# One inference step of a hybrid attention/RG-LRU layer on one core: values placed between zeros, a new order of the first loads and of the middle, and the last gate products on VectorE

## The chip, the cores and the metric

The kernel runs on one core of one Trainium2 chip. The core's engines are TensorE (PE, with its weight loads shown as PEld), VectorE (DVE), ScalarE (ACT), GpSimd (POOL) and SyncE (SP), which issues most DMAs. The metric is the device time of one execution in microseconds. Three runs of the kernel before took 758.29, 759.57 and 760.28 us, median 759.57.

## The reference, cut to what matters

One layer is computed for 512 latent tokens and 128 context tokens, all in float32. With `h` the normed and modulated input:

```
z = h @ w_in                                  # q, k, v, lx (LRU input), lg
attn  = windowed GQA (8 query heads, 2 key/value heads of 64, sink logit, 2-D rope);
        latent tokens also see the 128 cached context keys and values
xc    = conv4(lx);  r, ig = sigmoid(xc @ w_r), sigmoid(xc @ w_i)   # per direction
a     = exp(8 r log_sigmoid(lam));  u = sqrt(1 - a^2) * ig * xc
lru   = (forward scan of h = a h + u  +  backward scan) * gelu(lg)
x     = x + gate1 * rmsnorm([attn, lru] @ w_out)
h2    = rmsnorm(x) * (1 + scale2) + shift2
f     = relu(h2 @ w_up)^2 @ w_down
x     = x + gate2 * rmsnorm(f)
```

The outputs are both `x`, and the new keys, values and LRU states of the context. The attention step that the change touches is `einsum('bkgqs,bskd->bqkgd', p, v)`: for each of the two key/value heads, softmax weights times values, summed over blocks of 128 keys.

## The kernel before

The 640 tokens are columns; d_model is eight tiles of 128 partitions. A float32 product of large matrices is made of three products of rounded operands: each operand is split into a high part and a low part (`split`, `low` L231, `weight` L262), and high x high, high x low and low x high add up in one PSUM bank. Transposes, attention's weight-times-value products and the small products of the modulation stay plain float32.

The work comes in stages. A string START (L72) is a list of the first steps in strict order: loads of the input, of modulation weights (D, Q) and of input-projection weights (W), norms, modulation and the first input-projection tiles (m, h, b, z). A second string ORDER (L80) lists the middle: z are further tiles of the input projection, g0 to g3 the gates of the four LRU channel blocks (`lru_gates` L620: four 128x128 weights on two halves of 322 columns, each read out of PSUM by a sigmoid on ACT), x their decay (`lru_decay` L655: exp, tanh and square on ACT), q their scans (`lru_scan` L674: square root on ACT, then two scans on DVE), rope and keys the keys, vt the values (`do_values` L847), qs the query stacks, and u{g}{qb} ten attention units, one for each key/value head pair group g and query block qb. Then come the output projection, and the MLP: sixteen pairs of hidden tiles by a Strassen-like scheme of seven products (`up7` L1176), each followed by its part of the down projection (`down` L1262). At the last down, each of the five token tiles is finished (`out_part` L1239, `out_tile` L1249): square for the norm on ACT, product with the gate, scaled add to the residual, and the store.

ACT needs a table load whenever the kind of function changes: sigmoid, exp with tanh, square root. A table WORK (L38) gives for each kind of small work a string of letters, one per instance: a is ACT, d is DVE, p is POOL, s is a negated copy on ACT with an accumulating DMA issued by POOL, m a mixture. Behind START the order on each engine comes from the scheduler, which takes ORDER as priorities; the engines then run their lists in that order and wait for each other by semaphores. PSUM has eight banks: three z, two s, two t and one pv.

A unit (L772) makes scores for its keys on 64-row tiles, softmax on DVE and ACT, and then for each block of 128 keys four transposes into a bank t, one copy out of it, and the products with the values (L816). There the values of a block (`vblock` L765) are two tiles of 128x64: the product for half 0 writes PSUM partitions 0 to 63, that for half 1 partitions 64 to 127, each with 256 columns. A float32 product leaves two matmul records in the trace, one for each pass. Over ten units there are 30 such blocks.

Of the kernel before, what the change touches and what calls it, by code (L numbers as in the profile page):

```python
# [15 lines left out]
ALU = mybir.AluOpType  # L16
# [19 lines left out]


WORK = {  # L38
    "h_lo": "dpdddpdd",
    "lx_weight_lo": "pddp",  # L40
    "z_weight_hi": "ddddddaaaaaaaa",
    "z_weight_lo": "ddpppdddspdssd",
    "z_out": "aamadmamdmammm",
    "gate_weight_lo": "dddd",
    "lru_x_lo": "pdpp",
    "gated_x": "dpdpppdp",
    "gated_input": "dddppppp",
    "directions": "dppp",
    "rope_sin": "ppddd",
    "rope_cos": "pddpp",  # L50
    "rope_sum": "pdddd",
    "q_hi": "aaad",
    "q_lo": "dppd",
    "softmax_scale": "ammdamaddd",
    "softmax_turned": "daaaadaadadaddaadadddaaaaadaaadddaddadad",
    "attention_hi": "adaaaadaaa",
    "gelu_lo": "sssp",
    "w_out_hi": "ddaaddad",
    "w_out_lo": "ppppdpsdspppddpd",
    "norm_scaled": "adaaa",  # L60
    "h_whole": "dddddddd",
    "plain_lo": "pppp",
    "up_sums": "ddpd",
    "up_lo": "ddddddp",
    "up_square": "a",
    "down_lo": "pddp",
    "modulated": "daddddddddd",
}

START = """  # L72
    X3 X1 X0 Q1 X2 X4 X5 X6 Q3 Q0 X7 Q2 Q4 Q5 Q7 Da Q6 pt D1 a0 D0 tr dg a1 a2 a3 Db W0 D2 rb ac D3 m0 m1 b0 h0
    W1 m2 h1 b1 z00 b2 m3 z01 h2 h3 z20 z11 z30 W2 Ds z10 z31 b3 z21 bc z02 z22 s0 W3 m5 m4 z12 h4 z03 z32 m6
    z40 z13 s1 Dt z42 h5 z52 m7 h6 z41 z23 s2 h7 z51 t0 t1 z62 z33 t2 t3 z50 z43 s3 z61 z60 z72 sc z71 z53 tc
    z70 z63 z73
"""


ORDER = """  # L80
    z4 g0 z1 g1 m4 x0 rope m5 q0 keys x1 g2 z0 z5 q1 g3 qs0 vt x2 m6 z3 x3 q2 q3 qs1 m8 u00 z2 u01 m7 qs2 qs3
    u04 u11 z10 u12 m9 u03 g1d u10 u02 u13 z11 u14 z13 z12 l1 l2 l0 l3
"""
MOD_BANKS, GATE_BANKS, LX_BANKS = "tszztz", "sssz", "zszz"
MIX_BANKS, TURN_BANK = ("t", "t", "s", "s"), "z"

PLAIN = 2
SUMS = 0
RING = (0, 1, 7, 6, 2, 4, 3, 8, 5)
X1K, TK, KC = 0, (2, 4, 5), (4, 2)  # L90


class Arena:
# [59 lines left out]
def hybrid_step(ctx, tc, xT, xN, vecs, ropeT, ckT, cv, gw, modw, modg, win, wout, wup, wdown,  # L153
# [65 lines left out]
    def on(work, i):  # L219
        return engines[WORK[work][i]]  # L220
# [502 lines left out]
        evac(z_tile(ft), z.f, eng=WORK["z_out"][ft])  # L723
        return z

    vt, vb = blk.alloc(keep=True), blk.alloc(keep=True)
    ctxk = blk.alloc(keep=True)
    sp.dma_start(out=ctxk.f[:, :P], in_=ckT)
    sp.dma_start(out=vt.f[:, TOK - P : TOK], in_=cv)


    def keys(zk):

# [29 lines left out]
             (384, 384, 8, (2, 3, 4)), (768, 128, 9, (5,))]  # L763

    def vblock(b, g):  # L765
        if b == 5:
            return vb.f[:, 64 * g : 64 * g + 64]
        return vt.f[:, b * P + 64 * g : b * P + 64 * g + 64]

    ucol = [0]  # L770

    def unit(g, qb, qs):  # L772
        k0, n, m0, vbs = UNITS[qb]
        qc = slice(qb * P, (qb + 1) * P)
# [24 lines left out]
        dve.tensor_tensor(out=dn, in0=mn, in1=psink[:, 4 * g : 4 * g + 4], op=ALU.add)  # L799
        table("exp", act.activation(dn, dn, AF.Exp))  # L800
        dve.tensor_tensor(out=dn, in0=dn, in1=rs, op=ALU.add)
        dve.reciprocal(dn, dn)
        for j in range(4):
            if WORK["softmax_scale"][un] == "a" or (WORK["softmax_scale"][un] == "m" and j % 2):
                act.activation(S[j].f[:, :n], S[j].f[:, :n], AF.Copy, scale=dn[:, j : j + 1])
            else:
                dve.tensor_scalar(S[j].f[:, :n], S[j].f[:, :n], dn[:, j : j + 1], None, ALU.mult)
        pv = bank("pv")
        for b, vbk in enumerate(vbs):
            tr = bank("t")  # L810
            for pos, j in enumerate((0, 2, 1, 3)):
                pe.transpose(tr[:, pos * P : (pos + 1) * P], S[j].f[:, b * P : (b + 1) * P], idn)
            pt = blk.alloc()
            copy_on("softmax_turned", 4 * un + b, pt.f[:, :512], tr)
            for half in range(2):
                pe.matmul(pv[64 * half : 64 * half + 64, 0:256], vblock(vbk, half),  # L816
                          pt.f[:, 256 * half : 256 * half + 256], start=(b == 0), stop=(b == len(vbs) - 1))
            pt.free()
        for s in S:
            s.free()  # L820
        src = pv[:, 0:256].rearrange("p (k c) -> p k c", c=P)
        hv, lv = mixed[1][:, 2 * g : 2 * g + 2, qc], mixed[2][:, 2 * g : 2 * g + 2, qc]
        copy_on("attention_hi", un, hv.bitcast(F32R), src)
        dve.tensor_tensor(out=lv.bitcast(F32R), in0=src, in1=hv, op=ALU.subtract)
# [22 lines left out]
    def do_values():  # L847
        zv = zb[FT_V]
        for b0 in range(2):
            tr = bank("t")  # L850
            n = 4 if b0 == 0 else 1
            for b in range(n):
                pe.transpose(tr[:, b * P : (b + 1) * P], zv.f[:, (4 * b0 + b) * P : (4 * b0 + b + 1) * P], idn)
            dve.tensor_copy(vt.f[:, :512] if b0 == 0 else vb.f[:, :P], tr[:, : n * P])
        zv.free()
        sp.dma_start(out=v_o, in_=vb.f[:, :P])

    def do_unit(g, qb):
# [380 lines left out]
    def out_part(t, n, c, s):  # L1239
# [4 lines left out]
        if t == 4:  # L1244
            dve.tensor_tensor(out=g3b[1].f[:, c], in0=ac[t][:, c], in1=g3b[1].f[:, c], op=ALU.mult)
        else:
            pool.tensor_tensor(out=ac[t][:, c], in0=ac[t][:, c], in1=g3b[0].f[:, c], op=ALU.mult)

    def out_tile(t, s):  # L1249
        dve.tensor_tensor(out=s[:, 0:1], in0=s[:, 0:1], in1=s[:, 1:2], op=ALU.add)  # L1250
# [174 lines left out]
```

## Time and profile before

| what | value |
|---|---|
| median of three runs | 759.57 us |
| profiled execution, its own time | 758.07 us |
| its span | 754.8 us |
| PE busy | 715.4 us, 95% |
| DVE busy | 575.6 us, 76% |
| ACT busy | 397.3 us, 53% |
| POOL busy | 218.2 us, 29% |
| matmul records / table loads in the program | 4036 / 15 |
| DMA read / written | 89.34 / 5.40 MB |

The shares are averages over stages that differ. 0 to 28 us is the start, 28 to 93 modulation and input projection, 93 to 160 the LRU gates with the rest of the projection, 160 to 264 the attention units, 264 to 345 the output projection and the second norm, 345 to 740 the MLP, and the rest the last tiles' norms. A stage is read by the wait that ends last in it, not by the average. Start times in a timeline tell more than durations where TensorE is full, because matmuls overlap.

### The profile page before, as it was taken

The page shows a single profiled execution, that of the slowest core. Times are in us where ns is not written, and L with a number is a line of the kernel's source. Part 1 is how long each engine was busy: PE and PEld are TensorE (multiplying, and loading weights), DVE is VectorE, ACT ScalarE, POOL GpSimd, SP SyncE. Part 2 cuts the span into 40 slices and gives each one's busy share as a digit, 9 for nine tenths or more (in the row PEclk, how much of TensorE's full clock was granted, in tenths as well). Part 3 has the DMA queues.
Part 4 walks back from the last instruction along what each step waited for, and adds up shares of the span by engine and source line. Part 5 has one row for each costly group of instructions (what it writes and reads, how often), then busy time and mean ns, then how long its engine had stood idle before and what let it go on. Part 6 is the DMA issues. An engine that isn't in the chain of part 4 may idle for free. (4 is left out here: it accounts for less than half of the span.)

```text
span 754.8 us, 10989 instructions
## 1 busy us (share of the span) xinstructions
PE 715.4 (95%) x4036; PEld 593.0 (79%) x4036; DVE 575.6 (76%) x1011; ACT 397.3 (53%) x794; POOL 218.2 (29%) x179
## 2 busy tenths in 40 slices
PE   6899987999999999989999999999999999999992
PEld 2468876666666778789898998898899889888982
DVE  3736578776575648999999998786878778778568
ACT  6315598956555649746355345453544345344522
POOL 2302347641120343700321132033113303321323
PEclk9999999999999999999999999999999999999997
DMA  8953252757100797503423442033123203313403
GB/s 331 408 164 126 74 168 73 254 151 185 39 30 29 191 252 273 167 34 102 152 89 108 168 165 80 35 112 112 30 82 112 85 29 112 112 44 125 140 28 139
DMA packets 36837, 96.43 MB, mean 128 GB/s; under 512 B 11776, under 2 KB 12464, under 8 KB 36784
## 3 DMA queue, kind: packets, MB, share of 16 engines
q1 hardware_dynamic: 35760, 92.66, 36.3%
q0 software_dynamic: 1024, 3.08, 2.2%
q8 instruction: 31, 0.51, 0.3%
q14 instruction: 22, 0.18, 0.1%
HBM read 89.34 MB, written 5.40 MB: 126 GB/s over the span
## 5 line engine op out<-in xcount | busy, mean ns | idle before, releaser
L207 PE MATMUL ps_z<-rnd 128*128 128x320 f32 (+5 forms) x1756 | 298.8, 317 | 10.3 <-ACT big L207 4.6
L207 PEld LDWEIGHTS ps_z<-rnd 128*128 128x128 f32 x1756 | 270.2, 190 | 35.2 <-issue 11.0
L207 ACT CAST rnd<-big 128x512 fp32r<-128x512 f32 (+4 forms) x218 | 140.9, 657 | 221.7 <-PE ps_z L207 66.0
L1075 POOL TENSOR_TENSOR rnd<-big,rnd 128x512 fp32r<-128x512 f32 x54 | 84.2, 1572 | 277.3 <-ACT rnd L207 165.2
L207 ACT ACTIVATE big<-big 128x320 f32<-128x320 f32 (+7 forms) x221 | 111.8, 518 | 58.8 <-DVE big L207 55.2
L207 DVE TENSOR_TENSOR rnd<-big,rnd 128x512 fp32r<-128x512 f32 (+4 forms) x153 | 125.9, 828 | 11.5 <-ACT rnd L207 10.5
L207 PE MATMUL ps_s<-rnd,yt__1217 128*128 128x512 f32 (+1 forms) x438 | 117.7, 393 | 0.4 <-ACT yt__1217 L207 0.4
L207 PE MATMUL ps_t<-rnd,yt__1217 128*128 128x512 f32 x408 | 107.2, 394 | 0.0
L207 PEld LDWEIGHTS ps_s<-rnd,yt__1217 128*128 128x128 f32 x438 | 80.2, 188 | 16.1 <-ACT yt__1217 L207 0.7
L207 PEld LDWEIGHTS ps_t<-rnd,yt__1217 128*128 128x128 f32 x408 | 76.3, 188 | 17.2
L207 DVE TENSOR_TENSOR big<-big 128x512 f32<-128x512 f32 (+8 forms) x108 | 73.5, 685 | 14.9 <-ACT big L207 6.7
L207 PE MATMUL ps_s<-rnd 128*128 128x322 f32 (+6 forms) x312 | 70.8, 358 | 4.3 <-ACT big L207 3.2
L238 POOL TENSOR_TENSOR rnd<-big,rnd 128x1024 fp32r<-128x1024 f32 (+2 forms) x16 | 37.2, 2324 | 112.2 <-DVE rnd L207 33.0
L207 PEld LDWEIGHTS ps_s<-rnd 128*128 128x128 f32 (+1 forms) x312 | 46.2, 189 | 22.9 <-issue 8.9
L207 DVE TENSOR_TENSOR big<-big,ps_z 128x320 f32<-128x320 f32 x98 | 46.5, 480 | 16.0 <-PE ps_z L207 15.5
L207 DVE TENSOR_TENSOR big<-big,ps_t 128x512 f32<-128x512 f32 x60 | 40.9, 683 | 17.7 <-PE ps_t L207 17.1
L207 PE MATMUL ps_pv<-rnd,yt__1217 128*128 128x512 f32 (+1 forms) x204 | 53.4, 391 | 0.9 <-DVE yt__1217 L207 0.9
L207 DVE TENSOR_TENSOR big<-big,ps_s 128x512 f32<-128x512 f32 (+1 forms) x61 | 41.3, 677 | 16.2 <-PE ps_s L207 16.2
L207 PEld LDWEIGHTS ps_pv<-rnd,yt__1217 128*128 128x128 f32 x204 | 37.8, 188 | 9.9 <-DVE yt__1217 L207 1.4
L207 PE MATMUL ps_z<-tt__2709,rnd 128*128 128x320 f32 x224 | 41.4, 309 | 0.0
L207 PE MATMUL ps_t<-big 128*128 128x128 f32 (+4 forms) x236 | 37.3, 342 | 1.7 <-DVE ut__109 L207 1.1
L207 PEld LDWEIGHTS ps_z<-tt__2709,rnd 128*128 128x128 f32 x224 | 35.2, 188 | 0.0
(163 smaller groups left out, 714.8 us busy)
## 6 DMA issues: line engine op xcount, KB each, us to landing
big<-in_modw SPq DMA_DIRECT2D x32, 512.0 KB, 6.1
big<-in_wup SPq DMA_DIRECT2D x32, 512.0 KB, 3.3
big<-in_wdown SPq DMA_DIRECT2D x32, 512.0 KB, 4.3
big<-in_win SPq DMA_DIRECT2D x9, 512.0 KB, 6.1
xt__113<-in_modw SPq DMA_DIRECT2D x8, 512.0 KB, 10.4
big<-in_wout SPq DMA_DIRECT2D x16, 256.0 KB, 6.0
big<-in_wout SPq DMA_DIRECT2D x8, 512.0 KB, 4.9
big<-in_modg SPq DMA_DIRECT2D x8, 512.0 KB, 3.3
```

The source lines that it names most:

```text
L207: i = f(*a, **k)
L238: eng.tensor_tensor(out=lo, in0=src, in1=hi, op=ALU.subtract)
L1075: eng.tensor_tensor(out=self.l, in0=src, in1=self.b.f[:, :512], op=ALU.subtract)
```

## The change

Values: one block of three (instead of two) holds, for each block of 128 keys, 256 columns: values of head 0 (64 columns), 128 columns of zeros, values of head 1 (64). A slice of 128 columns is then either values and zeros or zeros and values. Both halves' products take 128x128 weights and write all 128 partitions, one adding to the other. POOL writes the zeros once; the cached values come by two DMAs instead of one and the new values leave by two.

START, ORDER and the letters of WORK are new, as are the order in which scratch blocks are given out and three indices of blocks. The gate products of tiles 0 to 3 in the last down (`out_part`) follow a new entry `out_gate` and stand on DVE.

```diff
     WORK (some of the entries that changed)
-    "gate_weight_lo": "dddd",
-    "lru_x_lo": "pdpp",
+    "gate_weight_lo": "spps",
+    "lru_x_lo": "pddd",
...
-    "softmax_scale": "ammdamaddd",
+    "softmax_scale": "ammmamadad",
...
-    "up_sums": "ddpd",
-    "up_lo": "ddddddp",
+    "up_sums": "dddd",
+    "up_lo": "ddpdpdd",
     "up_square": "a",
-    "down_lo": "pddp",
+    "out_gate": "dddd",
+    "down_lo": "pddd",
...
-    X3 X1 X0 Q1 X2 X4 X5 X6 Q3 Q0 X7 Q2 Q4 Q5 Q7 Da Q6 pt D1 a0 D0 tr dg a1 a2 a3 Db W0 D2 rb ac D3 m0 m1 b0 h0
+    X3 X0 X1 Q1 X4 X2 X5 X6 Q0 Q2 Q4 X7 Q3 Q5 Q6 Q7 pt Da D1 a0 tr a1 D0 dg a2 a3 Db D2 W0 rb D3 ac m0 m1 b0 h0
...
-    z4 g0 z1 g1 m4 x0 rope m5 q0 keys x1 g2 z0 z5 q1 g3 qs0 vt x2 m6 z3 x3 q2 q3 qs1 m8 u00 z2 u01 m7 qs2 qs3
+    g1 g0 z4 z1 m4 rope m5 x0 z0 keys q0 x1 g2 z5 g3 vt qs0 x2 q1 m6 z3 x3 q2 m8 q3 qs1 u00 z2 u01 m7 qs2 qs3
...
-    vt, vb = blk.alloc(keep=True), blk.alloc(keep=True)
+
+    vt = blk.alloc(3, keep=True)
+    vz = vt.f[:, : 6 * 2 * P].rearrange("p (b c) -> p b c", c=2 * P)
+
+    def vplaces(b, n):
+
+        return bass.AP(vz.tensor, vz[:, b, 0:64].offset, [list(vz.ap[0]), [2 * P, n], [192, 2], [1, 64]])
+
     ctxk = blk.alloc(keep=True)
     sp.dma_start(out=ctxk.f[:, :P], in_=ckT)
-    sp.dma_start(out=vt.f[:, TOK - P : TOK], in_=cv)
+    pool.memset(vz[:, :, 64:192], 0.0)
+    for g in range(2):
+        sp.dma_start(out=vz[:, 4, 192 * g : 192 * g + 64], in_=cv[:, 64 * g : 64 * g + 64])
...
     def vblock(b, g):
-        if b == 5:
-            return vb.f[:, 64 * g : 64 * g + 64]
-        return vt.f[:, b * P + 64 * g : b * P + 64 * g + 64]
+        return vz[:, b, P * g : P * g + P]
...
             for half in range(2):
-                pe.matmul(pv[64 * half : 64 * half + 64, 0:256], vblock(vbk, half),
-                          pt.f[:, 256 * half : 256 * half + 256], start=(b == 0), stop=(b == len(vbs) - 1))
+                pe.matmul(pv[:, 0:256], vblock(vbk, half), pt.f[:, 256 * half : 256 * half + 256],
+                          start=(b == half == 0), stop=(b == len(vbs) - 1 and half == 1))
...
         else:
-            pool.tensor_tensor(out=ac[t][:, c], in0=ac[t][:, c], in1=g3b[0].f[:, c], op=ALU.mult)
+            on("out_gate", t).tensor_tensor(out=ac[t][:, c], in0=ac[t][:, c], in1=g3b[0].f[:, c], op=ALU.mult)
```

On TensorE, before, around the first unit's first two key blocks (ps_pv is the unit's result, ps_t a bank of transposes, ps_s the next unit's scores):

```order
L207 MATMUL ps_s_1461<-rnd 128x128 [waits DVE_49]
L207 MATMUL ps_s_1461<-rnd 128x128 x2
L207 MATMUL ps_pv_1276<-big 64x256 [waits DVE_49]
L207 MATMUL ps_pv_1276<-big 64x256
L207 MATMUL ps_t_1293<-big 128x128 [waits PE_49]
L207 MATMUL ps_t_1293<-big,ut__109 128x128
L207 MATMUL ps_t_1293<-big 128x128
L207 MATMUL ps_pv_1276<-big 64x256 [waits Activation_49]
L207 MATMUL ps_pv_1276<-big 64x256
```

And at the same place after the change:

```order
L208 MATMUL ps_s_1469<-rnd 128x128 [waits DVE_49]
L208 MATMUL ps_s_1469<-rnd 128x128 x2
L208 MATMUL ps_z_1581<-rnd 128x384
L208 MATMUL ps_pv_1281<-big 128x256 [waits DVE_49]
L208 MATMUL ps_pv_1281<-big 128x256
L208 MATMUL ps_pv_1281<-big 128x256 [waits Activation_49]
L208 MATMUL ps_pv_1281<-big 128x256
L208 MATMUL ps_t_1298<-big 128x128 [waits PE_49]
L208 MATMUL ps_t_1298<-big,ut__109 128x128
```

The products write 128 partitions instead of 64; here the first two blocks, which stood around four transposes, now stand together. The count of matmuls is the same, 3833.

On ACT, before, from the end of gate block 2 into gate block 3 (results read out of PSUM with 322 columns are sigmoids; the pair of 644 columns are square roots):

```order
L207 ACTIVATE xt__113<-ps_s_886,big 128x322
L207 ACTIVATE xt__113<-ps_s_891,big 128x322
L207 ACT_TABLE_LOAD
L207 ACTIVATE big<-big 128x644 x2
L207 ACT_TABLE_LOAD
L207 ACTIVATE big<-ps_z_1032,big 128x322
L207 CAST rnd<-ut__109 128x640
L207 ACTIVATE big<-ps_z_1037,big 128x322
```

And after the change, at the same gates:

```order
L208 ACTIVATE xt__113<-ps_s_932,big 128x322
L208 ACTIVATE big<-ps_s_937,big 128x322
L208 ACTIVATE big<-ps_z_1025,big 128x322
L208 ACTIVATE big<-ps_s_942,big 128x322
L208 ACTIVATE xt__113<-ps_s_947,big 128x322
L208 ACTIVATE big<-ps_z_1030,big 128x322
L208 ACTIVATE xt__113<-ps_s_952,big 128x322
L208 ACTIVATE xt__113<-ps_z_1035,big 128x322
```

The two table loads and the square roots between the gate blocks are gone from here and stand further back, where decay of block 2, its square roots and decay of block 3 now follow one another with a load between each; the whole list has 15 loads in both.

On DVE, before, the last twelve instructions but the very end (sums with ps_pv and ps_s add a product to the result, the pairs of SCALAR_TENSOR_TENSOR are the scaled adds to the residual):

```order
L207 TENSOR_TENSOR big<-big,ps_pv_6405 128x256
L207 TENSOR_TENSOR big<-big 128x1
L207 TENSOR_TENSOR big<-big 128x512
L207 TENSOR_TENSOR big<-big,ps_s_6415 128x256
L207 TENSOR_TENSOR big<-big 128x256
L207 TENSOR_TENSOR big<-big 128x1
L207 RECIPROCAL big<-big 128x1
L207 TENSOR_TENSOR big<-big 128x256
L207 TENSOR_TENSOR big<-big 128x1
L207 SCALAR_TENSOR_TENSOR big<-big 128x512 x2
L207 RECIPROCAL big<-big 128x1
L207 SCALAR_TENSOR_TENSOR big<-big 128x512 x2
```

And a piece of the end after the change:

```order
L208 SCALAR_TENSOR_TENSOR big<-big 128x512 x2
L208 TENSOR_TENSOR big<-big,ps_t_6401 128x512
L208 TENSOR_TENSOR big<-big 128x512
L208 TENSOR_TENSOR big<-big,ps_pv_6411 128x256
L208 TENSOR_TENSOR big<-big 128x512
L208 TENSOR_TENSOR big<-big 128x1
L208 RECIPROCAL big<-big 128x1
L208 TENSOR_TENSOR big<-big,ps_s_6421 128x256
L208 TENSOR_TENSOR big<-big 128x512
L208 TENSOR_TENSOR big<-big 128x256
L208 TENSOR_TENSOR big<-big 128x1
L208 SCALAR_TENSOR_TENSOR big<-big 128x512 x2
```

The gate products of 128x512 now stand between the adds in DVE's list; before, only tile 4's product stood there.

## Rows read from the trace of the kernel before

**Rows 1.** The page's head

```profile
span 754.8 us, 10989 instructions
```

**Rows 2.** Windows: length, busy us of PE, PEld, DVE, ACT, POOL; clock, DMA, GB/s

```profile
93.00:160.00 67.00, 58.69 (x375) 45.08 (x374) 51.92 (x69) 57.03 (x95) 42.36 (x41) 0.97 0.54 172
160.00:264.00 104.00, 102.63 (x610) 70.69 (x609) 69.46 (x179) 61.70 (x150) 18.08 (x12) 1.00 0.34 94
264.00:345.00 81.00, 75.69 (x400) 65.00 (x401) 65.29 (x111) 50.99 (x99) 31.33 (x20) 1.00 0.59 181
345.00:400.00 55.00, 55.00 (x301) 48.87 (x300) 55.00 (x87) 24.17 (x47) 11.49 (x8) 1.00 0.36 123
...
124.70:128.00 3.30, 3.30 (x12) 2.93 (x12) 3.30 (x2) 2.22 (x5) 3.22 (x3) 0.50 0.25 61
```

**Rows 3.** Timeline around V products: start, us, engine, line, operation, out<-in, tile, form, count

```profile
165.72 0.27 PE L207 MATMUL ps_t<-big,ut__109 128*128 128x128 f32 x1
165.83 0.27 PE L207 MATMUL ps_t<-big 128*128 128x128 f32 x1
166.03 0.65 PE L207 MATMUL ps_pv<-big 128*64 128x256 f32 x4
166.61 0.33 PE L207 MATMUL ps_t<-big 128*128 128x128 f32 x1
...
228.21 0.65 PE L207 MATMUL ps_pv<-ut__109,big 128*64 128x256 f32 x4
229.22 0.62 PE L207 MATMUL ps_z<-rnd 128*128 128x384 f32 x2
```

**Rows 4.** The tile ps_pv: count, duration ns min/median/max, first and last start, forms

```profile
L207 PE MATMUL ps_pv<-big x82: 272/379/430, 18.9 to 263.3; 128*64 128x256 f32 x80, 128*128 128x128 f32 x2
L207 PE MATMUL ps_pv<-ut__109,big x40: 379/379/431, 171.4 to 252.0; 128*64 128x256 f32 x40
```

**Rows 5.** Timeline, plain float32 in the full shape

```profile
17.97 1.13 PE L207 MATMUL ps_s<-big 128*128 128x512 f32 x2
18.93 0.38 PE L207 MATMUL ps_pv<-big 128*128 128x128 f32 x2
```

**Rows 6.** Timeline, PE at the two longest waits behind the start

```profile
111.88 0.56 PE L207 MATMUL ps_s<-rnd 128*128 128x322 f32 x2 [2.74 <-ACT big L207]
...
123.50 0.70 PE L207 MATMUL ps_z<-rnd 128*128 128x322 f32 x3 [3.53 <-ACT big L207]
```

**Rows 7.** Timeline, ACT ahead of the second of them

```profile
118.94 1.28 ACT L207 ACT_TABLE_LOAD   x1
```

**Rows 8.** Timeline, DVE and ACT ahead of the first unit's products

```profile
148.78 2.98 DVE L207 TENSOR_TENSOR_SCAN big<-xt__113,big 128x643 f32<-128x643 f32 x1 [0.22 <-POOL xt__113 L677]
...
157.19 1.12 ACT L207 ACTIVATE big<-big 128x384 f32<-128x384 f32 x2 [2.55 <-DVE big L207]
```

**Rows 9.** Timeline, PE in the start

```profile
27.77 0.44 PE L207 MATMUL ps_z<-rnd 128*128 128x384 f32 x1 [1.23 <-ACT rnd L207]
```

**Rows 10.** Groups of instructions from 345 to 740: count, busy us, mean ns, idle before

```profile
L1187 POOL TENSOR_TENSOR big<-big 128x512 f32<-128x512 f32 x13 | 21.5, 1655 | 30.0 <-DMA big<-in_wup 28.9 <-DVE rnd L207 1.1
...
L207 DVE TENSOR_TENSOR big<-big 128x512 f32<-128x512 f32 x40 | 40.5, 1013 | 6.1 <-DMA big<-in_wup 5.8
```

**Rows 11.** Timeline of the end

```profile
733.02 1.56 PE L207 MATMUL ps_pv<-rnd,yt__1217 128*128 128x512 f32 x6
...
736.81 0.68 DVE L207 TENSOR_TENSOR big<-big,ps_pv 128x512 f32<-128x512 f32 x1
...
738.32 4.23 POOL L1247 TENSOR_TENSOR big<-big 128x512 f32<-128x512 f32 x3 [1.98 <-ACT big L207]
...
739.56 3.53 DVE L207 SCALAR_TENSOR_TENSOR big<-big 128x512 f32<-128x512 f32 x2
...
740.69 0.87 PE L207 MATMUL ps_s<-rnd,yt__1217 128*128 128x256 f32 x6
...
750.33 1.42 DVE L207 SCALAR_TENSOR_TENSOR big<-big 128x512 f32<-128x512 f32 x2
```

More of the change, by code (lines that the diff above doesn't have):

```diff
@@ L38 @@
 WORK = {
[L39 to L43, printed above, removed]
-    "gate_weight_lo": "dddd",
-    "lru_x_lo": "pdpp",
-    "gated_x": "dpdpppdp",
-    "gated_input": "dddppppp",
+    "h_lo": "dddddppd",
+    "lx_weight_lo": "pppp",
+    "z_weight_hi": "ddddddaaddaaaa",
+    "z_weight_lo": "ddspddppppdpsd",
+    "z_out": "aamamdmmdmmmmd",
+    "gate_weight_lo": "spps",
+    "lru_x_lo": "pddd",
@@ L48 @@
+    "gated_x": "dppddpdp",
+    "gated_input": "dddpdppp",
     "directions": "dppp",
-    "rope_sin": "ppddd",
-    "rope_cos": "pddpp",
+    "rope_sin": "pdddd",
+    "rope_cos": "pddpd",
     "rope_sum": "pdddd",
-    "q_hi": "aaad",
+    "q_hi": "ddda",
     "q_lo": "dppd",
-    "softmax_scale": "ammdamaddd",
[L55 to L59, printed above, removed]
@@ L60 @@
-    "norm_scaled": "adaaa",
+    "softmax_scale": "ammmamadad",
+    "softmax_turned": "daaaadaaaadaddaadadddaaaaadaaaaddaddadad",
+    "attention_hi": "addaaaaaad",
+    "gelu_lo": "sssd",
+    "w_out_hi": "ddadadaa",
+    "w_out_lo": "pdspdpsdppppddpd",
+    "norm_scaled": "adadd",
     "h_whole": "dddddddd",
     "plain_lo": "pppp",
-    "up_sums": "ddpd",
-    "up_lo": "ddddddp",
+    "up_sums": "dddd",
+    "up_lo": "ddpdpdd",
     "up_square": "a",
-    "down_lo": "pddp",
-    "modulated": "daddddddddd",
+    "out_gate": "dddd",
@@ L68 @@
+    "down_lo": "pddd",
+    "modulated": "daddddddadd",
 }
 START = """
-    X3 X1 X0 Q1 X2 X4 X5 X6 Q3 Q0 X7 Q2 Q4 Q5 Q7 Da Q6 pt D1 a0 D0 tr dg a1 a2 a3 Db W0 D2 rb ac D3 m0 m1 b0 h0
-    W1 m2 h1 b1 z00 b2 m3 z01 h2 h3 z20 z11 z30 W2 Ds z10 z31 b3 z21 bc z02 z22 s0 W3 m5 m4 z12 h4 z03 z32 m6
-    z40 z13 s1 Dt z42 h5 z52 m7 h6 z41 z23 s2 h7 z51 t0 t1 z62 z33 t2 t3 z50 z43 s3 z61 z60 z72 sc z71 z53 tc
-    z70 z63 z73
+    X3 X0 X1 Q1 X4 X2 X5 X6 Q0 Q2 Q4 X7 Q3 Q5 Q6 Q7 pt Da D1 a0 tr a1 D0 dg a2 a3 Db D2 W0 rb D3 ac m0 m1 b0 h0
@@ L77 @@
+    W1 m2 m3 h2 h1 b1 z00 Ds b2 h3 z20 z30 z01 z10 z31 b3 W2 bc s0 z21 z02 z22 z11 m5 W3 m4 z32 z12 h4 z03 m6 Dt
+    z40 z13 s1 h5 z52 m7 h7 z42 h6 s2 t0 z51 z23 z41 t1 t2 z62 z33 t3 z50 z43 s3 z72 sc z61 z60 tc z71 z53 z70
+    z63 z73
 """
 ORDER = """
-    z4 g0 z1 g1 m4 x0 rope m5 q0 keys x1 g2 z0 z5 q1 g3 qs0 vt x2 m6 z3 x3 q2 q3 qs1 m8 u00 z2 u01 m7 qs2 qs3
-    u04 u11 z10 u12 m9 u03 g1d u10 u02 u13 z11 u14 z13 z12 l1 l2 l0 l3
+    g1 g0 z4 z1 m4 rope m5 x0 z0 keys q0 x1 g2 z5 g3 vt qs0 x2 q1 m6 z3 x3 q2 m8 q3 qs1 u00 z2 u01 m7 qs2 qs3
@@ L83 @@
+    u04 u11 z10 u02 m9 u12 u10 g1d u03 u13 u14 z13 z11 l0 l3 z12 l1 l2
 """
@@ L88 @@
 SUMS = 0
-RING = (0, 1, 7, 6, 2, 4, 3, 8, 5)
-X1K, TK, KC = 0, (2, 4, 5), (4, 2)
+RING = (0, 1, 7, 5, 6, 2, 4, 3, 8)
+X1K, TK, KC = 4, (0, 1, 3), (4, 2)
 class Arena:
@@ L853, in do_values @@
                 pe.transpose(tr[:, b * P : (b + 1) * P], zv.f[:, (4 * b0 + b) * P : (4 * b0 + b + 1) * P], idn)
-            dve.tensor_copy(vt.f[:, :512] if b0 == 0 else vb.f[:, :P], tr[:, : n * P])
+            dve.tensor_copy(vplaces(5 * b0, n),
+                            tr[:, : n * P].rearrange("p (b g d) -> p b g d", g=2, d=64))
         zv.free()
-        sp.dma_start(out=v_o, in_=vb.f[:, :P])
+        for g in range(2):
+            sp.dma_start(out=v_o[:, 64 * g : 64 * g + 64], in_=vz[:, 5, 192 * g : 192 * g + 64])
     def do_unit(g, qb):
@@ L864, in do_unit @@
         if len(units) == 10:
-            for b in (*kk, vt, vb):
+            for b in (*kk, vt):
                 b.free()
```

## The prediction

> **What bounds the kernel now.** I began with the page's head and the profiled execution's own time: span 754.8 us [rows 1] inside 758.07 us, so 3.27 us lie around the span. The median of the runs shown is 759.57 us, 1.50 above the profiled one. I add the changes up against 758.07 and carry the sum over to 759.57.
>
> Then I cut the span into stages and asked for the busy time of each engine in each [rows 2]. Read PE's column first. From 160 to 264 us (attention units with filler products) PE is busy 102.63 of 104 us, from 345 to 400 all of 55: there TensorE sets the time, and an edit of its instructions counts in full. VectorE is full as well in 345 to 400, which matters for every operation handed to it. From 93 to 160 us PE has 58.69 of 67 us, with ACT at 57.03 and DVE at 51.92: nobody is full, a chain between engines sets the pace. From 264 to 345 PE lacks 5.3 us, spread over small waits. PE's last six products end at 741.56, DVE's last pair at 751.75 [rows 11]: the end is DVE's.
>
> **V products (PE-bound, 160 to 264).** The forms of this tile [rows 4] give 80 + 40 = 120 records of 128x64 weights on 256 columns; a key block leaves 4 (two halves, two passes each), so there are 30 blocks. What one costs is read from start to start. Transposes in the full shape follow each other after 0.11 us (165.72 to 165.83); the V group starts 0.20 after the last one, and the next instruction 0.58 after the group's start [rows 3]. So a lone block takes 0.09 + 0.58 = 0.67 us although its four passes are recorded with 256 columns each: the halves stand on different columns of the array and run beside each other, and what is lost is the change of shape on both sides. The interval behind the group is 0.06 to 0.15 longer than usual, I take 0.10. Two blocks in a row take 0.09 + 1.01 = 1.10 (228.21 to 229.22) [rows 3]. The trace has 22 lone blocks and 4 such doubles: 22 x 0.67 + 4 x 1.10 + 26 x 0.10 = 21.7 us.
>
> After the change a block has four passes of 256 columns behind each other, in the full shape. No row shows just this. Nearest is a run of fp32 transposes, 0.11 us for 128 columns, so 0.22 for 256, at which weights are changed every time as here; from above, two fp32 passes of 512 columns with their start took 18.93 - 17.97 = 0.96 us, 0.48 each, 0.24 for 256 [rows 5]. A block costs 0.87 to 0.96 us, thirty 26.2 to 28.8. I take the transposes' 26.2: 4.5 us more than now. Bounds: +4.5 to +7.1. From below, if each block hid one pass, 30 x 0.22 = 6.6 us would go and the edit would gain 2.1; no row supports that.
>
> Other changes of shape (scores on 64 rows, the modulation's 32-column tiles, gate transposes): by the two orders PE changes shape 176 times before, 52 of them at V groups, and 129 times after. The 124 others become 129; five at about 0.07 us give +0.3. V and shapes: **+4.8 us**.
>
> The trace speaks for both of two rules in the Trainium skill, "TensorEngine Tiling (Array Packing)", section Key Properties. One is "Mode switching requires drain", which is the reason for a change like this one; the other is "Tiles operate independently", by which the two halves' passes overlap. The rows agree with both: 0.20 instead of 0.11 us on entry, and four passes within 0.58 us. By the first alone V's sum would turn into a gain; the other keeps it at a loss.
>
> **Tail.** At the end DVE decides. The rows show POOL's gate products of 128x512 (three in 4.23 us from 738.32) beside DVE's scaled adds: two took 3.53 us at 739.56, while two with POOL idle took 1.42 at 750.33 [rows 11]. Gate products of tiles 0 to 3 go to DVE. In its new order, from the add of the last-but-one 512-column product in bank pv to the end, stand five adds of 512 columns, six gate products (one of them, tile 4's, stood there before), ten scaled adds, four instructions of 256 columns and nine on one column. At start-to-start prices (adds and gate products 0.60, since the add at 736.81 is followed at once, scaled adds 0.68, 256 columns 0.35, one column 0.07) that is 3.0 + 3.6 + 6.8 + 1.4 + 0.6 = 15.4 us. Now that stretch takes 736.81 to 751.75, 14.9 us; but the add needn't start at 736.81, when a contended pair lets it through: its product's six passes start at 733.02 and take 1.56 us [rows 11], so 734.6 is possible. End 750.0: **-1.8 us**. Gate products as dear as scaled adds make that -1.3; small ones for nothing, -2.4.
>
> **Middle (93 to 160).** The longest wait of the page is 3.53 us before 123.50, for ACT [rows 6]: ACT loads a table at 118.94 (1.28 us) [rows 7], takes two square roots, loads again, and only then reads the gate bank. The new ACT order has the sigmoids of both last gate groups in one piece, so this hole closes. Behind it the granted clock is 0.50 (1.2 GHz) from 124.7 to 128.0 [rows 2], after PE had lain nearly idle since 119.7; 3.3 us of work at half speed lose 1.7. At best 3.5 + 1.7 = 5.2 us are won. Against it: the number of table loads is 15 in both orders, so two of 1.28 us move to where decay and square roots of the two groups follow each other, on the way to the first unit's softmax. DVE is late there: scans such as the 2.98 us one at 148.78 make ACT's scaling at 157.19 wait 2.55 us for it [rows 8]. If everything comes back, the stage costs 2.6 more. The wait of 2.74 us at 111.88 [rows 6] stays, since the group's first sigmoid still stands behind a table load. Between -5.2 and +2.6 I take **-2.0**: two of the scans now stand behind scores instead of ahead of them, but most of ACT's work is only moved.
>
> **Start.** First loads change places, not the number of bytes. PE's largest wait there is 1.23 us before 27.77, for ACT's rounding [rows 9]; three smaller ones precede it. I take -0.5, bounds -1.5 and +1.5: one such wait gone or new.
>
> **MLP and late mix.** The third of the four Strassen sums per pair goes from POOL (1.66 us each [rows 10]) to DVE; two roundings' low parts go back to POOL, one comes. A 512-column sum on DVE averages 1.01 us beside POOL [rows 10]. DVE gains about 14 such instructions, POOL loses twice as many, and each that POOL loses frees DVE of contention. PE waits for nothing there, so I put it at 0; cover: operands prepared ahead of PE. If the cover goes in 345 to 450, where DVE has no slack, it costs up to 4 x 1.0 = 4 us. Output projection weights' and norms' new engines meet 5.3 us of PE waits [rows 2]: 0, bounds -2 and +2.
>
> **Sum:** +4.8 - 1.8 - 2.0 - 0.5 + 0 = +0.5 us: 758.6 on the profiled execution's basis, 760.1 on the median's. A measurement of this kernel can tell about 0.3%, 2.3 us, from no change; so the forecast is no change.
>
> **Rivals.**
> 1. The middle closes for good, and the late waits with it: hole 3.5 and clock 1.7 are both won and 2 more of the late 5.3: 759.57 + 4.8 - 1.8 - 5.2 - 0.5 - 2 = 754.9. For it: ACT is idle 10 of 67 us in this stage [rows 2], so its work could move together. Against it: equal table loads, and the wait only has to move to one of the other engines.
> 2. The V edit is itself the gain: the 26 V groups lose what the change of shape costs on both sides (0.09 + 0.10 us), while the passes take no longer than now. 26 x 0.19 = 4.9 us saved instead of 4.5 paid gives 759.57 - 4.9 + 0.3 - 1.8 - 2.5 = 750.7. Against it: 0.67 us for a lone block hold that change already, and four passes at 0.22 are more. The Trainium skill's first rule above, on drains, would speak for this case.
> 3. Slower: V's 4.8 us fall due in full, since PE has no gap from 160 to 264 to hide them, and the middle gives back what it saved, because two table loads stand on the way to the first unit. It decides once the softmax of that unit comes later than PE's fillers last: 759.57 + 4.8 - 1.8 + 0 to 2.6 = 762.6 to 765.2.
> 4. DVE becomes the bound of the first MLP pairs: 4 us on the forecast, 764.1. For it: the full column of 345 to 400 [rows 2]; against it: PE waits for nothing there.
>
> **How the numbers follow.** Forecast 0.36 (757.3 to 761.8, the band of no change); rival 1 0.26; rival 2 0.07; rival 3 0.22; rival 4 0.09. Faster is rivals 1 and 2, 0.33; slower 3 and 4, 0.31. The range takes in the forecast, rival 1 at 754.9 with a little room, and rivals 3 and 4 to 765.5: 753.5 to 765.5.
>
> **What would show it.** Right: V groups with 128x128 weights and 0.87 us per block, without the 0.20 on entry; PE still without gaps to the end of the units, this stage some 4 us longer; no wait near 123 us and no half clock behind it; scaled adds in the tail at 0.7 us throughout and DVE's end about 8.4 us behind PE's last product (741.56) instead of 10.2. Wrong: blocks at 0.7 us or below; a new wait of over 2 us between the last gates and the first unit; PE waiting for DVE after 345.

## The result: slower by 0.8%, and the profile after

Twelve runs of each kernel gave 765.05 us for the changed kernel (763.61 to 768.12) and 760.34 us for the kernel before (756.03 to 763.22); the ratio is 1.0079 with a 95% interval of 1.0055 to 1.0102, some 6.0 us (4.2 to 7.8; the two medians by themselves differ by 4.7). The time lies inside the range, but "no change" was the forecast and 0.31 the chance of slower. It is nearest to rival 3, which had 762.6 to 765.2.

The profiled execution of after took 768.0 us, near the upper end of its twelve, and that of before 758.07, below the median of its own. Setting these two side by side overstates the loss by about 4 us (9.9 against 6.0), so the main readings below are compared with a second execution of the same instruction lists, from an experiment whose edit touches the end only.

The stages of after, with the same columns as [rows 2]; the last two lines are stretches right behind long waits:

```profile
93.00:160.00 67.00, 57.86 (x373) 47.66 (x373) 59.46 (x78) 55.20 (x90) 32.77 (x33) 0.90 0.57 161
160.00:264.00 104.00, 102.00 (x581) 79.86 (x580) 69.04 (x182) 63.10 (x151) 17.65 (x17) 1.00 0.32 88
264.00:345.00 81.00, 75.24 (x354) 62.06 (x353) 55.26 (x101) 50.21 (x96) 30.21 (x18) 0.98 0.63 197
345.00:400.00 55.00, 54.65 (x321) 49.44 (x321) 55.00 (x86) 26.14 (x51) 16.21 (x6) 1.00 0.30 97
...
115.40:120.30 4.90, 4.90 (x22) 4.90 (x23) 2.46 (x3) 2.40 (x6) 3.11 (x3) 0.50 0.35 64
145.20:151.00 5.80, 5.74 (x21) 5.30 (x22) 4.87 (x12) 5.77 (x10) 2.23 (x5) 0.50 0.24 97
```

In the units TensorE is as busy as before, 102.00 against 102.63 of 104 us, but gets through 581 records instead of 610: on the mean each takes longer, which a busy share cannot show (the products beside V in the window differ somewhat, too). In the middle the granted clock fell from 0.97 to 0.90.

The V products of after in a timeline of TensorE:

```profile
174.64 0.93 PE L208 MATMUL ps_z<-rnd 128*128 128x258 f32 x5
175.41 1.02 PE L208 MATMUL ps_pv<-big 128*128 128x256 f32 x4
176.27 0.60 PE L208 MATMUL ps_t<-big 128*128 128x128 f32 x4
176.62 0.48 PE L208 MATMUL ps_z<-rnd 128*128 128x258 f32 x2
```

From 175.41 to 176.27 four passes take 0.86 us; the forecast had 0.87, against 0.67 before [rows 3]. The entry is free of the stall that stood there. Next to scores on 64 rows most blocks take 0.96 to 1.06 us, and the mean of all 30, waits left out, is 0.90. The long waits of TensorE in the middle of after, which answer to [rows 6]:

```profile
115.40 1.17 PE L208 MATMUL ps_s<-rnd 128*128 128x322 f32 x3 [3.98 <-ACT ut__109 L208]
...
145.26 1.87 PE L208 MATMUL ps_s<-rnd 64*128 64x384 f32 x6 [3.59 <-DVE big L208]
```

The wait near 123 us is gone, as forecast, because the sigmoids of both gate blocks run in one piece. But the one ahead of the gate block grew from 2.74 to 3.98 us, and a new one of 3.59 us stands ahead of the first unit's scores. What ACT did during the first (a cast and a scaled copy, both 128x512, round gate weights):

```profile
112.35 0.62 ACT L208 CAST rnd<-big 128x512 fp32r<-128x512 f32 x1
112.87 0.63 ACT L208 ACTIVATE rnd<-big 128x512 fp32r<-128x512 f32 x1
113.52 1.28 ACT L208 ACT_TABLE_LOAD   x1
114.82 0.53 ACT L208 ACTIVATE ut__109<-ps_s,big 128x322 f32<-128x322 f32 x1
```

The scaled copy is the letter s in the new `gate_weight_lo`; DVE made this low part before, and the cast stood elsewhere in ACT's list. Before, the table load followed the last such work directly:

```profile
109.26 0.72 ACT L207 ACTIVATE big<-xt__113 128x644 f32<-128x644 f32 x1
110.00 1.28 ACT L207 ACT_TABLE_LOAD   x1
```

The two roundings take 1.2 us, from 112.35 to 113.52, between the last exp work and the table load that TensorE waits for; from the table load ahead of that exp work to the sigmoid ACT needs 7.97 us instead of 6.87, and the wait is 1.24 us longer. And DVE ahead of the second wait:

```profile
140.05 2.74 DVE L208 TENSOR_TENSOR_SCAN ut__109<-xt__113,big 128x643 f32<-128x643 f32 x1
...
143.19 1.50 DVE L208 TENSOR_TENSOR_SCAN big<-xt__113 128x643 f32<-128x643 f32 x1 [0.34 <-POOL xt__113 L686]
144.61 0.59 DVE L208 CUSTOM_DVE_ANT_0 big<-ps_s,big 128x384 f32<-128x384 f32 x1
```

Two scans stand in front of the instruction that reads the first scores out of PSUM at 144.61; until it has read them the next scores have no bank. The forecast counted on scans standing behind the scores; two do, and these two do not.

The end of after, which answers to [rows 11]:

```profile
752.74 1.41 DVE L208 SCALAR_TENSOR_TENSOR big<-big 128x512 f32<-128x512 f32 x2
753.10 0.87 PE L208 MATMUL ps_s<-rnd,yt__1242 128*128 128x256 f32 x6
754.67 0.69 DVE L208 TENSOR_TENSOR big<-big 128x512 f32<-128x512 f32 x1
...
760.98 1.42 DVE L208 SCALAR_TENSOR_TENSOR big<-big 128x512 f32<-128x512 f32 x2
```

Scaled adds cost 0.70 us throughout, and DVE ends 760.98 + 1.42 - 753.97 = 8.4 us behind TensorE, where it was 10.2.

### The profile page after: what moved, and what is told of

It reads as the page before. It is cut to its first block, busy times and chain, and to the rows that moved or that the text cites. A ratio compares the mean times of both kernels' runs of the same rounds, so it can differ in the third digit from the quotient of the medians.

```text
span 766.0 us, 10981 instructions
## 1 busy us (share of the span) xinstructions
PE 724.1 (95%) x4036; PEld 612.8 (80%) x4036; DVE 561.7 (73%) x1034; ACT 400.0 (52%) x800; POOL 180.4 (24%) x154
## 5 line engine op out<-in xcount | busy, mean ns | idle before, releaser
L208 PE MATMUL ps_z<-rnd 128*128 128x320 f32 (+5 forms) x1756 | 302.6, 319 | 8.7 <-DMA rnd<-in_wout 2.9
L208 PEld LDWEIGHTS ps_z<-rnd 128*128 128x128 f32 x1756 | 273.9, 192 | 30.7 <-issue 8.0
L208 ACT CAST rnd<-big 128x512 fp32r<-128x512 f32 (+2 forms) x221 | 143.2, 659 | 227.2 <-PE ps_z L208 85.5
L208 ACT ACTIVATE big<-big 128x320 f32<-128x320 f32 (+7 forms) x241 | 123.6, 531 | 65.3 <-DVE big L208 63.0
L208 DVE TENSOR_TENSOR rnd<-big,rnd 128x512 fp32r<-128x512 f32 (+5 forms) x154 | 119.6, 789 | 20.0 <-PE ps_s L208 9.9
L208 DVE TENSOR_TENSOR big<-big 128x512 f32<-128x512 f32 (+8 forms) x135 | 81.6, 619 | 16.3 <-DMA big<-in_wup 7.4
L208 PE MATMUL ps_t<-big 128*128 128x128 f32 (+3 forms) x283 | 40.9, 327 | 3.0 <-DVE big L208 2.9
L208 DVE CUSTOM_DVE_ANT_0 big<-ps_s,big 128x512 f32<-128x512 f32 (+2 forms) x37 | 22.7, 619 | 19.7 <-PE ps_s L208 13.7
```

The source lines that it names most:

```text
L208: i = f(*a, **k)
```

## The experiments

The theory after the result: V costs 4 to 5 us and the tail returns 1.8, both as forecast; the new lists of the middle do not win 2.5 us but lose 3 to 4, through waits that moved and through TensorE's clock behind them. The rivals: V carries the whole loss; or V costs nothing and the lists carry it all.

For each profiled execution I added up TensorE's time from start to start: waits (idle ended by another engine or a DMA, over 0.15 us), what the clock cost (half of the time at 1.2 GHz in which it did not wait), the V groups (with their entry and exit), and the rest. The clock's column moves by up to 0.4 us with how the edges of a stretch are counted. Times in us; the ratio is that of the timed runs.

| kernel | ratio to before | first V | last V | PE end | waits | clock | V | rest |
|---|---|---|---|---|---|---|---|---|
| before | 1 | 165.0 | 263.3 | 741.6 | 19.7 | 3.4 | 19.8 | 692.3 |
| before, gates on DVE | 0.9948 | 165.4 | 263.8 | 746.6 | 23.0 | 6.8 | 19.8 | 690.6 |
| before, wide V | 1.0101 | 166.3 | 263.2 | 751.5 | 22.2 | 9.3 | 27.3 | 686.3 |
| before, new places, narrow V | 1.0041 | 165.2 | 258.2 | 744.4 | 22.9 | 4.9 | 19.1 | 691.1 |
| after | 1.0079 | 169.2 | 269.9 | 754.0 | 21.5 | 9.2 | 27.9 | 687.2 |
| after, gates on POOL | 1.0105 | 167.3 | 268.2 | 752.3 | 21.7 | 7.6 | 27.9 | 687.1 |
| after, narrow V | 1.0073 | 167.2 | 267.0 | 752.0 | 25.1 | 11.8 | 19.2 | 688.1 |
| after, old V | 1.0025 | 167.3 | 262.6 | 746.7 | 23.5 | 6.8 | 19.5 | 689.2 |
| after, old ORDER | 1.0067 | 166.5 | 262.3 | 753.1 | 23.2 | 8.2 | 27.5 | 686.5 |

**Only the gate products on DVE** (kernel before).

```diff
-            pool.tensor_tensor(out=ac[t][:, c], in0=ac[t][:, c], in1=g3b[0].f[:, c], op=ALU.mult)
+            on("out_gate", t).tensor_tensor(...)      # "out_gate": "dddd"
```

> The kernel before with one edit: the gate products of tiles 0 to 3 in the last down stand on VectorE. All lists of instructions are the same up to the last tiles. Theory (the prediction's tail term holds): DVE ends about 8.4 us behind TensorE's last product instead of 10.2, ratio to before 0.9976 (-1.8 us). Rival (DVE only takes over what POOL did beside it): DVE's end moves by less than 0.5 us, ratio 1.000.

Measured: 0.9948, interval 0.9911 to 0.9984. The end of its trace:

```profile
745.73 0.87 PE L208 MATMUL ps_s<-rnd,yt__1217 128*128 128x256 f32 x6
...
753.60 1.41 DVE L208 SCALAR_TENSOR_TENSOR big<-big 128x512 f32<-128x512 f32 x2
```

755.01 - 746.60 = 8.4 us, as forecast: in the trace the tail is worth 1.8 us. The timed gain, 4.0 us with an interval of 1.2 to 6.8, agrees with that but is too wide to confirm the size. This is the fastest kernel of the study and beats both. Its lists equal those of before up to the last tiles, so it also shows how the same program varies: its TensorE waited for the DMA of output-projection weights like this,

```profile
282.20 3.30 PE L208 MATMUL ps_z<-rnd 128*128 128x512 f32 x7 [4.38 <-DMA rnd<-in_wout]
```

while the wait at this place was 0.71 us in the execution of before, which is most of why that one looks so quick (PE end 741.6 against 746.6). In after it was 2.91. This wait differs between executions and is no part of the change's price.

**Only the wide V** (kernel before with values between zeros; the edits of the change's diff on `vz`, `vplaces`, `vblock` and `unit`).

> The kernel before with only the values between zeros; START, ORDER and all letters as before, the scheduler places the rest. Theory (V is a pure cost): 0.86 us per key block instead of 0.67 to 0.78, so +4.5 us, ratio 1.006. Rival (the whole loss of the change is its new order, V costs nothing): ratio 1.000. Rival (V carries the whole loss): ratio 1.010 with the tail's 1.8 us not yet taken off.

Measured: 1.0101, interval 1.0047 to 1.0154. That is the last rival's number (the theory's 1.006 lies in the interval as well), but the scheduler also placed the rest anew, from about 70 us on, so the next run takes the products by themselves.

**New places, narrow V** (against the run before this one only the products differ).

```diff
-                pe.matmul(pv[:, 0:256], vblock(vbk, half), pt.f[:, 256 * half : 256 * half + 256],
-                          start=(b == half == 0), stop=(b == len(vbs) - 1 and half == 1))
+                pe.matmul(pv[64 * half : 64 * half + 64, 0:256], vz[:, vbk, 192 * half : 192 * half + 64],
+                          pt.f[:, 256 * half : 256 * half + 256], start=(b == 0), stop=(b == len(vbs) - 1))
```

> The kernel before with the new places of the values in memory and the zeros, but products of 64 columns that write 64 partitions each. Against the run with wide products alone only the products differ; the lists agree up to the first unit's products. Theory (four full passes per block cost more than the two shape changes): V and its neighbours take about 4 us less TensorE time than with wide products, ratio to before 1.004 against 1.010. Rival (the loss of that run comes from the lists that the scheduler made anew, not from the products): ratio 1.010.

Measured: 1.0041, interval 1.0013 to 1.0070, against 1.0101. The difference, 0.6% or 4.6 us, is the theory's number, but the two intervals together leave some 0.6% to either side of it. The windows of the units' stage, wide first, then narrow:

```profile
170.00:270.00 100.00, 97.32 (x555) 77.58 (x554) 65.95 (x163) 55.70 (x136) 17.47 (x11) 0.97 0.33 96
```

```profile
170.00:270.00 100.00, 98.00 (x581) 68.31 (x580) 64.02 (x164) 57.18 (x136) 19.99 (x12) 1.00 0.35 99
```

Nearly equal busy time, 26 records fewer. That is not V's price alone: the wide window holds 6.8 us at 1.2 GHz (hence its 0.97), which makes up more than half of it. By the table, which takes the clock out, V needs 27.3 instead of 19.1 us, and the rest falls by 4.8, with 117 changes of shape instead of 156: net +3.4 us of TensorE time. The new places and the lists that follow from them cost another 0.4%.

**After with narrow V** (the same edit in the kernel after).

> The kernel after with one edit: the products read the 64 columns of values alone and write 64 partitions each, as before; everything else as after, lists the same up to the first unit's products. Theory (V 4.5 us of the loss, the rest waits and half clock in the middle, which are the same here): ratio to before 1.002, the first V group at the same time as in the kernel after, the stretch from first to last V group 4 us shorter. Rival (V costs nothing beside other work): ratio 1.008 as after.

Measured: 1.0073, interval 1.0040 to 1.0105; first V at 167.2 us, where after had 169.2 and its second execution 167.3; first to last V 99.8 us instead of 100.7. This expectation failed: the two kernels differ by 0.06%, with some 0.4% to either side. V did fall by 8.7 us in the table, but waits rose by 3.6 and the clock's cost by 2.6, and the rest by 0.9: in these lists, which the scheduler then made differently behind the first unit, TensorE came early to instructions that were not ready. TensorE time is a bound only as long as the others keep up.

**After with the old V in every respect** (two blocks, no zeros; the rest as after).

> The kernel after with the values as before in every respect (two blocks, products of 64 columns, no zeros); START, ORDER, letters and gate products on VectorE as after. Theory (V 4 to 5 us, middle and clock the rest): ratio to before 1.001 to 1.003. Rival (the new order of the middle carries the loss): ratio 1.008.

Measured: 1.0025, interval 0.9994 to 1.0056, as the theory had it. So V, its places and the lists that follow from them carry 1.0079 - 1.0025 = 0.54%, 4.1 us, with some 0.4% to either side. What remains, 0.25% or 1.9 us, holds the tail's gain of 1.8 already: by this subtraction START, ORDER and the letters lose 3.7 us (1.3 to 6.1) where the forecast had them win 2.5. It doesn't say where. The lists of this kernel and of after part at about 70 us, and after's two long waits are not in it; its longest from 93 to 170 us are of 2.05 and 1.82 us and this one:

```profile
156.30 0.97 PE L208 MATMUL ps_s<-rnd 64*128 64x512 f32 x3 [3.27 <-DVE big L208]
```

**After with the gate products on POOL.**

```diff
-    "out_gate": "dddd",
+    "out_gate": "pppp",
```

> The kernel after with the last gate products of tiles 0 to 3 on POOL as before; all lists equal to those of after up to the last tiles, so it also shows how far the profiled execution of after is typical. Theory (tail 1.8 us): ratio to before 1.010, DVE ends 10 us behind TensorE's last product. If the long waits of after (about 4.0 us for ACT at the third gate block, 3.6 us for DVE at the first scores) belong to its order, they are here within 0.7 us, with a stretch at 1.2 GHz behind each; if chance made them, at least one is under 2 us.

Measured: 1.0105, interval 1.0061 to 1.0150: 0.26% or 2.0 us more than after, the theory's number, with some 0.5% to either side. Two scaled adds take 3.52 us again beside POOL's products, and DVE ends 10.15 us behind TensorE. The waits of the middle, and the stretches behind them:

```profile
113.48 1.17 PE L208 MATMUL ps_s<-rnd 128*128 128x322 f32 x3 [3.99 <-ACT ut__109 L208]
143.37 1.86 PE L208 MATMUL ps_s<-rnd 64*128 64x384 f32 x6 [3.56 <-DVE big L208]
```

```profile
113.30:118.50 5.20, 5.02 (x22) 5.02 (x23) 2.44 (x3) 2.58 (x7) 3.27 (x4) 0.50 0.34 61
...
143.30:149.20 5.90, 5.83 (x21) 5.40 (x22) 4.93 (x14) 5.87 (x10) 2.33 (x5) 0.50 0.24 97
```

Same waits to 0.03 us, same half clock. So that two such waits come belongs to the lists of after. The length of the first and the clock behind it vary, though: in the kernel with narrow V and in the one with a busy TensorE (below), whose lists are those of after up to there, it was

```profile
113.94 0.71 PE L208 MATMUL ps_s<-rnd 128*128 128x322 f32 x3 [3.12 <-ACT ut__109 L208]
115.19 0.71 PE L208 MATMUL ps_s<-rnd 128*128 128x322 f32 x3 [3.13 <-ACT ut__109 L208]
```

with 3.4 us at 1.2 GHz behind the first of these and none behind the second:

```profile
115.00:118.30 3.30, 3.30 (x18) 3.30 (x17) 2.36 (x3) 1.34 (x3) 2.04 (x1) 0.50 0.46 79
115.20:122.00 6.80, 6.80 (x48) 6.41 (x49) 4.80 (x10) 5.04 (x12) 3.11 (x3) 1.00 0.57 115
```

ACT needs the same time in all four; TensorE came 0.9 us later to the wait here, counted from ACT's table load. The second wait is 3.58 us with narrow V, with 6.8 us at half clock as above.

**A busy TensorE in the second wait** (16 products of the identity with itself ahead of the first unit's scores, placed behind the last product of modulation m8).

```diff
+        if un == 0:
+            busy(16, ends[108])      # pe.matmul(d[:, :P], idn, idn), 16 times
         for h, l in qs:
```

> The kernel after with 16 products of the identity by itself (128 columns, float32, about 3.5 us, results not used) in TensorE's list at the place where it waits 3.6 us for DVE ahead of the first unit's scores. They add no work that anything waits for. Theory (the wait itself makes the clock fall): no stretch at 1.2 GHz behind this place (6.8 us in the profile of after), and about 2.9 us less than after, ratio to before 1.004. Rival (the clock falls at that time for another reason, or the stretch costs nothing since ACT and DVE set the pace): clock still 0.5 there, or ratio 1.008 as after.

Measured: 1.0142, interval 1.0083 to 1.0202, so the expected time failed. Its trace:

```profile
139.51 3.62 PE L208 MATMUL ps_pv<-big 128*128 128x128 f32 x30
...
163.98 0.69 PE L208 MATMUL ps_t<-big 128*128 128x128 f32 x2 [7.10 <-ACT big L208]
```

```profile
142.80:147.00 4.20, 1.88 (x20) 1.30 (x20) 3.34 (x7) 4.18 (x8) 2.42 (x5) 1.00 0.40 164
...
164.00:175.00 11.00, 10.67 (x33) 8.12 (x34) 4.65 (x14) 6.92 (x17) 0.76 (x2) 0.50 0.73 239
```

Behind the filled place the clock stays at full speed, where after and the kernel with the gate products on POOL had half. But the scheduler, which counts the extra products, made the lists behind them anew, with z fillers earlier; TensorE then lay idle for 7.10 us ahead of the unit's transposes, and the half clock came there. So the wait had only moved once more, and what one would gain with TensorE kept busy and nothing else changed was not measured.

**After with the old ORDER.**

> The kernel after with the string ORDER as before; START, letters, values and gate products as after. Theory (the middle's new order loses about 3 us by waits and clock): ratio to before 1.003 to 1.005, first V group 2 us or more earlier than after's 169 us. Rival (ORDER is not it: V, or the letters): ratio 1.008 or above and first V group at 168 us or later.

Measured: 1.0067, interval 1.0038 to 1.0096, first V at 166.5. The units end 6 to 8 us earlier than in the two executions of after's lists (262.3 against 269.9 and 268.2), but TensorE's end is the same, 753.1 against 754.0 and 752.3: fillers stand later, and the time with them. The interval holds the theory's 1.004 to 1.005 and the rival's 1.008 alike, so whether ORDER carries a part of the loss is not decided; the trace shows no gain at TensorE's end.

**After with the old letters, and before with the new START** (the second also with the gate products on DVE).

> The kernel after with the table WORK as before (and the gate products on VectorE as after); START, ORDER and values as after. Theory (V 4 us, tail -2, and some 3 to 4 us from the new lists, most of it waits and half clock that any new placing of the middle brings): ratio to before 1.003 to 1.008. Rival (the letters are the cause of the rest): ratio 1.003 or less and no wait of over 2.5 us from 93 to 170 us.

> The kernel before with the new string START and the last gate products on VectorE; no other edit. If both terms of the prediction hold: ratio to before 0.997 (-0.5 and -1.8 us) and faster than both kernels. If START only changes what the scheduler finds afterwards, the 360th matmul starts within 0.7 us of the kernel before (70.4 us there without a stretch of half clock in the start, 71.6 to 72.2 with one), and the time is that of the run with the gate products alone or up to 4 us above.

Measured: 1.0209 (1.0167 to 1.0251) and 1.0146 (1.0096 to 1.0196). Both expectations were too low: START or the letters of one kernel with the rest of the other are worse than either. The 360th matmul, by which the second kernel's START was to be read, starts at 74.5 us, at least 2.3 later than in the lists of before, so that part failed as well; in the first kernel, which has the new START too, it starts at 75.3. With the old letters only one rounding, the cast, stands ahead of the table load at the third gate block, and the wait there is 2.60 us (ACT needs 7.44 us where it was 7.97 with both and 6.87 with none):

```profile
113.98 0.62 ACT L208 CAST rnd<-big 128x512 fp32r<-128x512 f32 x1
114.61 1.28 ACT L208 ACT_TABLE_LOAD   x1
...
116.49 1.27 PE L208 MATMUL ps_s<-rnd 128*128 128x322 f32 x6 [2.60 <-ACT ut__109 L208]
```

Behind the second norm TensorE waits for POOL in both; TensorE's wait and POOL's instruction in the second kernel:

```profile
364.53 1.22 PE L208 MATMUL ps_t<-rnd,yt__1217 128*128 128x512 f32 x2 [6.35 <-POOL rnd L1076]
```

```profile
L1076 POOL TENSOR_TENSOR rnd<-big,rnd 128x512 fp32r<-128x512 f32 x1 | 18.6, 18557 | 16.9 <-ACT rnd L208 16.9
```

One low part of 128x512 took POOL 18.56 us, where three products of that size took 4.23 in the tail [rows 11]. The waits for POOL, 3.41 us in the first kernel and 6.35 in the second, are only a part of the 16 and 11 us that these kernels lose; where the rest goes was not followed. DVE ran two-operand work without a gap meanwhile. In after the longest such instruction took 8.1 us, and TensorE did not wait for it.

## Why the prediction was wrong

The failed step is the middle's -2.0 us. The prediction counted the gain of closing one wait and put what comes back at less than that. In the traces the waits and the clock's cost from 93 to 170 us rose by some 4.3 us instead, which is above the step's own upper bound of +2.6. Term by term:

- **V and shapes, forecast +4.8.** Right in mechanism and near in size. A block between products of the full shape costs 0.86 us (forecast 0.87). By the table TensorE's time in V and the rest together rises from 712.1 and 710.4 us in the two executions of the lists of before to 715.1 and 715.0 in those of after, some 3.8 us. Timed, the wide products cost 0.60% in the lists of before (1.0101 against 1.0041, with some 0.6% to either side) and, with their places and the lists that follow, 0.54% in those of after (1.0079 against 1.0025, some 0.4%): 4.6 and 4.1 us. The third pair (1.0079 against 1.0073, some 0.4%) doesn't show it; there waits took the place. So that the edit of the values costs time is shown, by the kernel before with this edit alone above all; how much of it the products take by themselves is shown in TensorE's time only.
- **Tail, forecast -1.8.** Right: DVE ends 8.4 us behind TensorE instead of 10.2 with the gate products on DVE, in both pairs of kernels. The timed differences, 0.26% and 0.52% with some 0.5% and 0.4% to either side, agree.
- **Middle, forecast -2.0 between -5.2 and +2.6.** Wrong in sign. The hole at 123.5 did close. But of the two long waits of before (2.74 and 3.53 us) the first grew to 3.98, mostly by the two roundings that ACT's new list puts ahead of its table load, and a second of 3.59 arose ahead of scores of the first unit, from two scans on DVE. The prediction took the first as unchanged without following ACT's list back beyond the table load, and did not see these two scans in front of the scores. Both stand in the order of instructions.
- **The clock** was the mis-sized part of the same step. I reckoned that 1.7 us of loss at 1.2 GHz would go with the hole. There are two stretches now, from 113.5 to 120.3 and 144.2 to 151.1 us, each behind one of the two waits; TensorE works 4.9 and 5.8 us at half speed in them, which loses 5.4 us. From 93 to 170 us waits and clock together took 10.0 and 11.5 us in the two executions of the lists of before, 15.4 and 14.7 in the two of after. First V starts 3.1 us later (168.3 against 165.2 as means of the pairs).
- **Start, forecast -0.5.** Slightly wrong: the 360th matmul starts at 72.2 and 71.6 us in the two executions of before's lists, at 72.7 and 70.7 in those of after; executions without half clock in the start compare at 70.4 (before, narrow V) and 70.7 to 71.2. So +0.3 to +0.8 rather than -0.5. TensorE's first product starts at 7.4 to 7.9 us in every kernel with the new START and at 6.2 in every one with the old; most of that is made up later.
- **MLP and late mix, forecast 0.** Held for the MLP: from its first product to TensorE's end 390.4 and 390.1 us in the lists of before, 390.8 and 390.5 in those of after. DVE's extra operations stay hidden; rival 4 did not come. The late mix varies more between executions of one program (wait for the DMA 0.71 or 4.38 us) than between the kernels.

In the traces V with shapes makes +3.8 us, waits and clock of the middle +4.3 and the tail -1.8, together 6.3 where 6.0 was measured. That they meet so closely is partly luck, since TensorE's waits differ by 3.3 us between the two executions of the lists of before alone. By timed kernels V's 4.1, the tail's -1.8 and 3.7 us for START, ORDER and letters are the 6.0 by construction: the 3.7 is what is left over.

That remainder is not the middle's 4.3 us, and the middle's loss does not belong to the new order alone. By the same addition waits and clock from 93 to 170 us take 14.0 and 13.9 us in the two kernels of before that have only the new places of the values (wide and narrow products), with START, ORDER and letters as before. With START, ORDER and letters new and the old values they take 12.1; with all of it new 15.4 and 14.7, and 13.7 with narrow products. So with the new places alone, whose lists part from those of before at 70 us, this stretch already loses about 3 us (one execution each), which the prediction had nowhere. How the loss divides among places, START, ORDER and letters stays open: exchanging any one of them also changed the lists. How much of it the clock makes and how much the waits is the table's reading only, since the one attempt to fill a wait changed the lists too.

Rival 3, with a chance of 0.22, had the right sum (V in full, the middle gives back what it saves) but another reason: it had two table loads on the way to the first unit, while the rows show two roundings, two scans and the clock. That its 762.6 to 765.2 comes so near is in part luck.

## What to carry to other kernels

Where an engine waits, follow the list of the engine it waits for back past the obvious instruction, in the new order, and add up what now stands in front; a hole closed in one place is often only refilled further on. Price a TensorE wait at its length, and allow for a stretch of half clock behind it, which mostly cost 1.5 to 3 us here but did not come behind every wait. When an edit makes a scheduler place everything anew, the kernel with that edit alone shows more than a list of its expected gains: here the new places of the values changed waits far from the products that they were made for. Before removing changes of shape, set the stall they cost against the passes that ran beside each other: here 0.67 us for two halves side by side beat 0.86 for four full passes, and only the neighbours paid part of it back.

## What the runs showed of the hardware

- The half clock doesn't follow from the length of a wait alone. With equal lists, a wait of 2.74 us at the third gate block was followed by full clock in one execution, and one of 2.14 us by a stretch of 3.4 us at 1.2 GHz in the other. What decides between them is open. In the lists of after the same wait was 3.98, 3.99, 3.12 and 3.13 us in four executions, with 6.8, 6.8, 3.4 and 0 us at half clock. In the start, one of two executions of after's lists had a stretch and the other none.

The wait of 2.14 us, the clock behind it, and the clock behind the one of 2.74 us:

```profile
110.90 1.73 PE L208 MATMUL ps_s<-rnd 128*128 128x322 f32 x6 [2.14 <-ACT big L208]
```

```profile
111.30:114.60 3.30, 3.30 (x17) 3.30 (x16) 2.00 (x3) 1.96 (x6) 3.26 (x2) 0.50 0.00 0
```

```profile
111.90:123.40 11.50, 8.07 (x56) 7.44 (x56) 8.01 (x10) 9.28 (x19) 8.76 (x5) 1.00 0.22 46
```

- DVE and POOL don't always share the loss. In the tail a scaled add took 1.77 us beside POOL's product instead of 0.70; behind the second norm DVE's two-operand instructions went on at about 0.67 us for 512 columns for some 14 us, and one POOL instruction took 18.56. The Trainium skill, "SBUF — State Buffer", section "Who interferes with whom", states that a DVE instruction with two inputs in SBUF contends with a GpSimd instruction that reads SBUF. Both places agree with it. At the second norm the loss fell on POOL alone over some twenty DVE instructions in a row.
